# Weights of an input projection loaded and split in pairs of blocks, with two kinds of scratch tile in one ring of slots

## The chip, the cores and the metric

The kernel runs on one core of a Trainium2 chip. The metric is the device time of one launch in microseconds (us). Each engine of the core (PE for matmuls, ACT, DVE and POOL for everything elementwise, SP for issuing transfers) works through its own queue of instructions in order; they wait for one another by semaphores.

## What is computed

One layer of a streaming encoder on a sequence of 1024 tokens with 1024 channels, all in float32:

```
h   = RMSNorm(x) * (1 + scale(c)) + shift(c)
z   = h @ w_in          # 256 q latent, 128 kv latent, 32 rotary key, 3 x 512 for chunk attention
A   = latent attention, 8 heads: q and k, v expanded from the latents, rotary part, QK norm,
      softmax over all keys up to the query's chunk of 64
B   = chunk attention, 8 heads of 64: QK norm, relative position bias,
      softmax over the query's chunk and the 8 chunks before it
x1  = x + gate(c) * (concat(A, B) @ w_out)
out = x1 + gate2(c) * (silu(conv3(g)) * conv3(u)) @ w_down,   [g, u] = h2 @ w_up,  h2 = modulated RMSNorm(x1)
```

The channel sizes of the last line are 1024 to 2 x 2816 and 2816 to 1024. The change concerns only how `w_in` comes to be used.

## The kernel before, in words

Every float32 product is done as three matmuls: each operand is split into a rounded part (hi) and the rest (lo), and hi x hi, hi x lo and lo x hi are summed (`gemm3`, L146 to L152). A weight is thus loaded by SP, copied to its hi part by ACT (`hi_of`, L75), and its lo part is a subtraction on POOL (`lo_of`, L82).

The work has these stages, by time: the start to about 94 us (x is loaded and normed, scale and shift are computed, h is transposed, and the first q and k columns are projected); chunk attention to about 410 us, with the rest of the input projection between its tiles; latent attention to 684 us, first with the expansion of the latents and then with the first half of the output projection between its tiles; the second half of the output projection to 790; the MLP to the end.

The two attentions run over units (a head pair or a head, half of the queries) of four tiles of 128 queries. For each tile `scores` makes the scores (`sc` or `sm`, L658), ACT the exponentials (`Pc` or `Pm`, L683), POOL and DVE their two half-precision parts (`hlc` or `hlm`, L71 and L703), a DMA their transpose (`PTc` or `PTm`, L705); three tiles later `values` multiplies them with v (`pvc` or `pvm`, L716). Between these, `pace` draws steps from a list of generators, the fillers, in this order: v0, qk1, qk2, v1, qk3 (columns of chunk attention: `f_v`, `f_qk`), m (the latents: `f_m`), up0, up1 (`f_up`: expansion of the latents for four heads each) and oca (`f_oca`: the output projection's part of chunk attention). The program's text only says what is drawn when; a planner then orders every engine's queue at build time by its estimate of times, and also decides which slot of a pool a tile gets. A tile that gets a used slot makes its first writer wait for the last reader of the tile before.

`load_w` (L170 to L191) loads one such set of weights, in eight blocks of 128 channels. For 256 columns (`w_qk` as `wq_r`, `w_v` as `wv_r`) each block is one DMA of 128 KB (L184) into one of three raw slots of 128x256, one ACT copy (L75) and one POOL subtraction (L82) of 128x256. For the latents' 416 columns (`wm_r`) each block is a piece of 256 and one of 160 columns, each with its own DMA, copy and subtraction. Where v's norm is needed (`ssw`), ACT also squares each block (L187); the squares' sums go through `pow2_scale` (L337 to L352, PE's part `vsp` at L341) to the scale that v is multiplied with, and `vsp` stands ahead of the projection of v (`ipv`).

Two kinds of scratch tile matter. `rtile` (L134) gives a tile of 128x512 out of four slots named "R": `raw` in `qk_norm` (L363 to L375), `lat` in `f_m` (L472 to L503), `uqr` and `kraw` in `f_up` (L553 and L569), `cl` and `ch` in `f_oca`. `qtile` (L137) gives one of the same size out of two slots named "sq": the squares `sq`, `msq`, `usq` and the discarded squares `wv_j`, but also the raw weights of `f_up` (`wqr` L526, `wkr` L532) and of the output projection (`wor`, `load_wo`), and the results `co` of `f_oca` (L610) until they are stored.

Of the kernel before, what the change touches and what calls it, by code (L numbers as in the profile page):

```python
# [12 lines left out]
F32 = mybir.dt.float32  # L13
F32R = mybir.dt.float32r
# [3 lines left out]
AF = mybir.ActivationFunctionType  # L18
# [5 lines left out]
P = 128  # L24
# [3 lines left out]
ND = D // P  # L28
# [34 lines left out]
def layer_kernel(ctx, tc, I, out):  # L63
    nc = tc.nc
    pe, act, dve, pool, sp = nc.tensor, nc.scalar, nc.vector, nc.gpsimd, nc.sync

    def f32(ap):
        return ap.bitcast(F32)
# [4 lines left out]
    def hi_of(eng, o, i):  # L73
        if eng == "a":
            act.activation(o, i, AF.Copy)  # L75
        elif eng == "p":
            pool.tensor_scalar(o, i, 1.0, 0.0, op0=MUL, op1=ADD)
        else:
            dve.tensor_copy(o, i)

    def lo_of(eng, o, i, hi):
        (pool if eng == "p" else dve).tensor_tensor(o, i, f32(hi), op=SUB)  # L82
# [39 lines left out]
    hw = right.__enter__()  # L122
    att_pg = tc.tile_pool(name="apg", bufs=1, side="left")
    apg = att_pg.__enter__()
# [7 lines left out]
    st = startp.__enter__()  # L132

    def rtile(name, shape=(P, 512), dt=F32):  # L134
        return apg.tile(list(shape), dt, name=name, tag="R", bufs=4)

    def qtile(name):  # L137
        return apg.tile([P, 512], F32, name=name, tag="sq", bufs=2)

    def atile(name):  # L140
        return apg.tile([P, 256], F32, name=name, tag="A", bufs=3)
# [27 lines left out]

    def load_w(name, src, ncol, he="a", ssw=None):  # L170
        tiles = []
        for k in range(ND):
            if ncol <= 256:
                w = hw.tile([P, 2, 256], F32R, name=f"{name}s{k}", tag="ws", bufs=16)
                hi, lo = w[:, 0, :ncol], w[:, 1, :ncol]
            else:
                wh = hw.tile([P, 512], F32R, name=f"{name}h{k}", tag="ws", bufs=16)
                wl = hw.tile([P, 512], F32R, name=f"{name}l{k}", tag="ws", bufs=16)
                hi, lo = wh[:, :ncol], wl[:, :ncol]
            for c0 in range(0, ncol, 256):  # L180
                c = slice(c0, min(c0 + 256, ncol))
                raw = hw.tile([P, 256], F32, name=f"{name}r{k}_{c0}", tag="wr", bufs=3)
                rw = raw[:, :c.stop - c0]
                sp.dma_start(rw, src[:, k, c])  # L184
                if ssw is not None:
                    junk = qtile(f"{name}j{k}")
                    act.activation(junk[:, :c.stop - c0], rw, AF.Square, accum_out=ssw[:, k:k + 1])  # L187
                hi_of(he, hi[:, c], rw)
                lo_of("p", lo[:, c], rw, hi[:, c])
            tiles.append((hi, lo))  # L190
        return tiles  # L191


# [15 lines left out]
    for t in range(NT):  # L209
        xt = xs[t]  # L210
        junk = st.tile([P, D], mybir.dt.bfloat16, name=f"xj{t}", tag="hv", bufs=2)
# [20 lines left out]

    hT = {}
    wqk = load_w("wq0_", I["w_qk"][0], 256)
    qk0 = [ps.tile([P, 1024], F32, name=f"qk0_{i}", tag="S", bufs=2) for i in range(2)]
    for d in range(ND):
        if d + 1 < ND:
            load_ada(d + 1)
        w = wada[d]
# [15 lines left out]
        for t in range(NT):  # L255
            h, j = divmod(t, 4)
# [106 lines left out]
    def qk_norm(src_psum, nm, qn, j0):  # L363

        raw = rtile(f"raw{nm}")
        act.activation(raw[:], src_psum, AF.Copy)
        sq = qtile(f"sq{nm}")
        act.activation(sq[:], raw[:], AF.Square)
        ss = cst.tile([P, 8], F32, name=f"ss{nm}", tag="ss", bufs=4)
        r = cst.tile([P, 8], F32, name=f"r{nm}", tag="rr", bufs=4)  # L370
        dve.tensor_reduce(ss[:], sq[:].rearrange("p (a b) -> p a b", a=8), axis=AX.X, op=ADD)
        rsqrt_mean(r[:], ss[:], HD)
        pool.tensor_tensor(qn[:, j0:j0 + 2, :].rearrange("p t (a b) -> p (t a) b", a=4),
                           raw[:].rearrange("p (a b) -> p a b", a=8),
                           r[:].unsqueeze(2).to_broadcast([P, 8, HD]), op=MUL)  # L375
# [10 lines left out]
    def f_qk(p):  # L386
        w = load_w(f"wq{p}_", I["w_qk"][p], 256)
        for h in range(2):
            qns[p, h] = pgtile([P, 4, 256], F32, f"qn{p}_{h}")
        for t in range(0, NT, 2):  # L390
            pt = ps.tile([P, 512], F32, name=f"ipq{p}_{t}", tag="mm", bufs=2)
            yield from proj2(pt, t, w, 256)
            qk_norm(pt[:], f"{p}_{t}", qns[p, t // 4], t % 4)

    def f_v(pp):
        ssw = cst.tile([P, ND], F32, name=f"ssw{pp}")
        w = load_w(f"wv{pp}_", I["w_v"][pp], 256, ssw=ssw)
        vscale["c", pp] = pow2_scale(f"c{pp}", ssw[:], hb[:], ND, 2.0 * D)
        sc = vscale["c", pp][0]
        for t in range(0, NT, 2):  # L400
            h, j = divmod(t, 4)
            if j == 0:
                for i in range(2):
                    vts[2 * pp + i, h] = apg.tile([P, 4, 2, 2, 64], F16, name=f"v{2 * pp + i}_{h}", tag="v16", bufs=6)
            pt = ps.tile([P, 512], F32, name=f"ipv{pp}_{t}", tag="mm", bufs=2)
            yield from proj2(pt, t, w, 256)
            for i in range(2):
                vt = vts[2 * pp + i, h][:, j:j + 2]
                src = pt[:].rearrange("p (t q a b) -> p t q a b", t=2, q=2, a=2)[:, :, i]
                act.activation(vt[:, :, :, 0, :], src, AF.Copy, scale=sc)  # L410
                dve.scalar_tensor_tensor(vt[:, :, :, 1, :], src, sc, vt[:, :, :, 0, :], op0=MUL, op1=SUB)
# [105 lines left out]
    def f_up(gr):  # L517
# [24 lines left out]
        for t in range(NT):  # L542
            h, j = divmod(t, 4)
            sl = slice(j * P, (j + 1) * P)
            if t % 2 == 0:
# [4 lines left out]
            yield from gemm3_f(pt[:, :384], [(latT[k, h][:, 0, sl], latT[k, h][:, 1, sl], wq[k][:, 0, :384], wq[k][:, 1, :384])  # L550
                                for k in range(2)])
            raw = rtile(f"uqr{gr}_{t}")
            act.activation(raw[:, :384], pt[:, :384], AF.Copy)  # L553
            sq = qtile(f"usq{gr}_{t}")
# [261 lines left out]
    tiles = [(u, i) for u in units for i in range(4 * u.g, 4 * u.g + 4)]  # L816
    for n in range(len(tiles) + DEPTH):
        if n < len(tiles):
            u, i = tiles[n]
# [4 lines left out]
        if n >= DEPTH:  # L824
            u, i = tiles[n - DEPTH]
# [47 lines left out]
    for t in range(NT):  # L873
        lo = gb.tile([P, 4, P], F32R, name=f"ol{t}", tag="ol", bufs=3)
        hi = gb.tile([P, 4, P], F32R, name=f"oh{t}", tag="oh", bufs=3)
# [19 lines left out]
        if t % 4 == 3:  # L895
            h = t // 4
# [32 lines left out]
    def mt(tag, shape, name, dt=F32):  # L929
        return mp.tile(list(shape), dt, name=name, tag=tag, bufs=MB[tag])  # L930
# [21 lines left out]
    def split(src, nm):  # L952
        w = mt("ws", [P, 2, 512], nm, F32R)
        hi_of("a", w[:, 0], src)
        lo_of("p", w[:, 1], src, w[:, 0])
        return w
# [59 lines left out]
    for h in range(2):  # L1016
# [4 lines left out]
        for j in range(NF):  # L1021
            raw = mt("raw", [P, D], f"wd{h}_{j}")
            sp.dma_start(raw[:], I["w_down"][j * P:(j + 1) * P, :])
            dve.tensor_tensor(raw[:], raw[:], gmbc[:], op=MUL)  # L1024
            w = [split(raw[:, n * 512:(n + 1) * 512], f"wds{h}_{j}{n}") for n in range(2)]
# [11 lines left out]
        for t in range(4):  # L1037
            xt = mt("u", [P, D], f"xo{h}{t}")
            sp.dma_start(xt[:], x1_d[4 * h + t])
            for n in range(2):  # L1040
                c = slice(n * 512, (n + 1) * 512)
# [76 lines left out]
```

## Time and profile before

| | |
|---|---|
| runs | 1496.44, 1496.47, 1498.27 us; median 1496.47 |
| profiled execution | 1497.56 us, of which the span from first to last instruction is 1495.8 |
| mean granted clock of PE | 0.918 |
| busy in the span | PE 1283.1 us (86%), DVE 1037.7 (69%), POOL 841.8 (56%), ACT 617.5 (41%) |
| DMA | 185.94 MB, mean 124 GB/s |

"Busy" is the time in which an engine has an instruction in work. Matmuls are pipelined and their ends are modelled, so a PE that is busy all the time need not be at its peak; the granted clock, given as a share of full speed, tells whether it was held back. The timeline gives for each instruction its start, its duration, engine, line, operation and the tiles it writes and reads; in brackets stands how long the engine was idle before it and what released it. A window row gives the busy times of a stretch of the span.

### The profile page before, as it was taken

To read this page: it belongs to the slowest core of one execution; us is meant where nothing else is said; L and a number is where in the kernel's file an instruction comes from. 1 tells how busy PE (TensorE), PEld (TensorE's weight loads), DVE (VectorE), ACT (ScalarE), POOL (GpSimd) and SP (SyncE) were. 2 spreads that over 40 slices of the span, in tenths; PEclk is the share of its full clock that TensorE was granted. 3 is DMA by queue.
4 is the path that set the end of the run, shared out by engine and by line. 5 is a ranking of instruction groups with operands and counts; after the bars stand their busy time and mean duration, and the time that the engine had idled before them with its cause. 6 is when DMAs were issued, how large, how long until landed. Compare 5 with 4: busy or idle time off the path is not lost.

```text
span 1495.8 us, 20236 instructions
## 1 busy us (share of the span) xinstructions
PE 1283.1 (86%) x6836; PEld 1063.9 (71%) x6836; DVE 1037.7 (69%) x1710; ACT 617.5 (41%) x1190; POOL 841.8 (56%) x860
## 2 busy tenths in 40 slices
PE   3859989998968788876829769999999999999997
PEld 2759868976747666655617558888888887887885
DVE  6864786466768768863576658887787788556553
ACT  4454353343546545532444224444444443332331
POOL 4264453373799845443766146665565555665663
PEclk9979988998878899987958979999999999999999
DMA  7323656464512668778411242222222234446442
GB/s 275 134 70 73 135 121 143 116 134 102 124 49 53 145 144 167 163 156 287 149 74 57 71 143 82 85 85 85 85 85 84 77 129 169 148 148 234 154 141 99
DMA packets 217443, 185.94 MB, mean 124 GB/s; under 512 B 147958, under 2 KB 182906, under 8 KB 216316
## 3 DMA queue, kind: packets, MB, share of 16 engines
q1 hardware_dynamic: 217340, 184.66, 43.0%
q8 instruction: 54, 0.88, 0.2%
q14 instruction: 49, 0.40, 0.1%
HBM read 121.17 MB, written 28.84 MB: 100 GB/s over the span
## 4 chain that ended last, share of the span: by engine, by line
PE 48%; DMA 16%; DVE 13%; POOL 12%; issue 7%; ACT 2%; SPq 1%; DVEq 0%; POOLq 0%; ACTq 0%
PE p L964 7%; PE p L962 7%; PE p L963 7%; POOL wds L82 4%; DMA aw<-w_ada 4%; DMA PTm<-hlm 3%; PE sc L658 3%; PE dnp L1034 2%; PE dnp L1036 2%; PE dnp L1035 2%; DVE adacc L243 1%; DMA wu<-w_up 1%; PE ipv L150 1%; DVE aacc L430 1%; PE pvc L716 1%
## 5 line engine op out<-in xcount | busy, mean ns | idle before, releaser
L82 POOL TENSOR_TENSOR wds<-wd,wds 128x512 fp32r<-128x512 f32 x88 | 153.5, 1763 | 100.2 <-ACT wds L75 100.2
L1034 PE MATMUL dnp<-wds,g 128*128 128x512 f32 x308 | 119.9, 391 | 4.3 <-DVE xo L1042 2.4
L1024 DVE TENSOR_TENSOR wd<-wd,gmbc 128x1024 f32<-128x1024 f32 x44 | 69.4, 1578 | 77.7 <-DMA wd<-w_down 77.7
L1035 PE MATMUL dnp<-wds,g 128*128 128x512 f32 x308 | 119.7, 389 | 0.0
L1036 PE MATMUL dnp<-wds,g 128*128 128x512 f32 x308 | 118.5, 390 | 0.5 <-DVE g L82 0.5
L75 ACT ACTIVATE wds<-wd 128x512 fp32r<-128x512 f32 x88 | 54.6, 624 | 152.0 <-PE dnp L1036 149.6
L71 POOL TENSOR_SCALAR hlm<-Pm,rim 128x512 f16<-128x512 f32 (+4 forms) x88 | 61.7, 704 | 71.6 <-DMA PTm<-hlm 53.9
L703 DVE SCALAR_TENSOR_TENSOR hlm<-Pm,rim,hlm 128x512 f16<-128x512 f32 (+4 forms) x88 | 69.7, 795 | 31.7 <-POOL hlm L71 31.4
L71 POOL TENSOR_SCALAR hlc<-Pc,ric 128x640 f16<-128x640 f32 (+2 forms) x64 | 45.5, 713 | 77.9 <-DVE ric L686 38.7
L82 POOL TENSOR_TENSOR wc<-ws,wc 128x512 fp32r<-128x512 f32 x22 | 50.8, 2311 | 64.9 <-ACT wc L75 64.9
L82 POOL TENSOR_TENSOR wa<-wu,wa 128x512 fp32r<-128x512 f32 x22 | 35.9, 1633 | 91.1 <-ACT wa L75 91.1
L970 DVE SCALAR_TENSOR_TENSOR u<-c,pk,u 128x1023 f32<-128x1023 f32 x44 | 75.6, 1725 | 4.1 <-ACT u L969 4.1
L82 DVE TENSOR_TENSOR g<-gr,g 128x512 fp32r<-128x512 f32 x44 | 70.9, 1613 | 8.8 <-ACT g L75 8.8
L683 ACT ACTIVATE Pc<-sc,mc 128x640 f32<-128x640 f32 (+2 forms) x64 | 42.2, 659 | 83.6 <-DVE mc L673 66.9
L658 PE MATMUL sm<-mk,mq 96*128 96x512 f32 (+3 forms) x288 | 70.2, 378 | 7.0 <-ACT Pm L683 6.5
L716 PE MATMUL pvm<-PTm,vt 128*128 128x128 f16 x576 | 50.6, 242 | 29.4 <-DMA PTm<-hlm 25.3
L658 PE MATMUL sc<-k,q 64*128 64x512 f32 (+3 forms) x288 | 69.8, 370 | 5.6 <-ACT Pc L683 3.7
L430 DVE SCALAR_TENSOR_TENSOR aacc<-aw,cs,aacc 128x256 f32<-128x256 f32 x84 | 45.5, 541 | 41.8 <-DMA aw<-w_ada 41.2
L716 PEld LDWEIGHTS <-vt 128*128 128x128 f16 x576 | 41.2, 110 | 42.8 <-issue 40.0
L1034 PEld LDWEIGHTS dnp<-wds,g 128*128 128x128 f32 x308 | 57.8, 188 | 18.0 <-DVE xo L1042 3.3
L1036 PEld LDWEIGHTS dnp<-wds,g 128*128 128x128 f32 x308 | 57.8, 188 | 13.5 <-DVE g L82 1.4
L971 DVE SCALAR_TENSOR_TENSOR u<-c,pk,u 128x1022 f32<-128x1022 f32 x44 | 66.8, 1554 | 0.0
(352 smaller groups left out, 4350.8 us busy)
## 6 DMA issues: line engine op xcount, KB each, us to landing
wu<-w_up SPq DMA_DIRECT2D x44, 512.0 KB, 3.5
wd<-w_down SPq DMA_DIRECT2D x44, 512.0 KB, 3.5
aw<-w_ada SPq DMA_DIRECT2D x96, 128.0 KB, 2.3
g_d<-u SPq DMA_DIRECT2D x22, 512.0 KB, 2.6
gr<-g_d SPq DMA_DIRECT2D x44, 256.0 KB, 3.1
x<-x SPq DMA_DIRECT2D x16, 512.0 KB, 7.4
adaw<-w_ada_a SPq DMA_DIRECT2D x8, 1024.0 KB, 4.9
wq_r<-w_qk SPq DMA_DIRECT2D x32, 128.0 KB, 2.4
```

Of the source, the lines that this page charges most:

```text
L71: pool.tensor_scalar(o, i, s, 1.0, op0=MUL, op1=MUL)
L82: (pool if eng == "p" else dve).tensor_tensor(o, i, f32(hi), op=SUB)
L658: last = pe.matmul(s[:, c:c + w], qpg[rs_, a, q], kpgs[kh][rs_, b, ko:ko + w], start=(a == 0 and b == 0), stop=(a == 1))
L703: dve.scalar_tensor_tensor(hl[:, w:2 * w], pp, ri[:], hl[:, :w], op0=MUL, op1=SUB)
L716: last = pe.matmul(u.pv[:, c], u.vst(j), mov, start=(x == 0), stop=(x == len(todo) - 1))
L962: pe.matmul(pt, sh, pg[:, 0], start=(k == 0), stop=False)
L963: pe.matmul(pt, sh, pg[:, 1], start=False, stop=False)
L964: pe.matmul(pt, sl, pg[:, 0], start=False, stop=(k == 3))
L970: dve.scalar_tensor_tensor(u[:, 1:], c[:, :S - 1], pk[:, cv + 1:cv + 2], u[:, 1:], op0=MUL, op1=ADD)
L1034: pe.matmul(pts[t][n], sh, w[n][:, 0], start=(j == 0), stop=False)
L1035: pe.matmul(pts[t][n], sh, w[n][:, 1], start=False, stop=False)
L1036: pe.matmul(pts[t][n], sl, w[n][:, 0], start=False, stop=(j == NF - 1))
```

## The change

`load_w` treats two blocks of channels at a time when there are at most 256 columns, and one block of 416 columns whole otherwise. A raw tile is now 128x512 (two blocks of 256 columns side by side), with two slots in place of three of half the size. There is one DMA, one hi copy and one lo subtraction for a pair; the squares stay one for each block. The hi and the lo part are tiles of their own, of 128x512, in the same sixteen slots as before. The three raw slots of 1 KB in each partition become two of 2 KB. `rtile` and `qtile` now draw from one ring, "R", of five slots; before there were four and two. In the whole program ACT, POOL and SP have 32 instructions fewer each; PE and DVE have as many as before, in a new order in the stages up to the output projection.

```diff
     def rtile(name, shape=(P, 512), dt=F32):
-        return apg.tile(list(shape), dt, name=name, tag="R", bufs=4)
+        return apg.tile(list(shape), dt, name=name, tag="R", bufs=5)

     def qtile(name):
-        return apg.tile([P, 512], F32, name=name, tag="sq", bufs=2)
+        return apg.tile([P, 512], F32, name=name, tag="R", bufs=5)
...
     def load_w(name, src, ncol, he="a", ssw=None):
         tiles = []
-        for k in range(ND):
-            if ncol <= 256:
-                w = hw.tile([P, 2, 256], F32R, name=f"{name}s{k}", tag="ws", bufs=16)
-                hi, lo = w[:, 0, :ncol], w[:, 1, :ncol]
-            else:
-                wh = hw.tile([P, 512], F32R, name=f"{name}h{k}", tag="ws", bufs=16)
-                wl = hw.tile([P, 512], F32R, name=f"{name}l{k}", tag="ws", bufs=16)
-                hi, lo = wh[:, :ncol], wl[:, :ncol]
-            for c0 in range(0, ncol, 256):
-                c = slice(c0, min(c0 + 256, ncol))
-                raw = hw.tile([P, 256], F32, name=f"{name}r{k}_{c0}", tag="wr", bufs=3)
-                rw = raw[:, :c.stop - c0]
-                sp.dma_start(rw, src[:, k, c])
-                if ssw is not None:
-                    junk = qtile(f"{name}j{k}")
-                    act.activation(junk[:, :c.stop - c0], rw, AF.Square, accum_out=ssw[:, k:k + 1])
-                hi_of(he, hi[:, c], rw)
-                lo_of("p", lo[:, c], rw, hi[:, c])
-            tiles.append((hi, lo))
+        n = 2 if ncol <= 256 else 1
+        for k in range(0, ND, n):
+            raw = hw.tile([P, n, 512 // n], F32, name=f"{name}r{k}", tag="wr", bufs=2)[:, :, :ncol]
+            sp.dma_start(raw, src[:, k:k + n, :])
+            if ssw is not None:
+                for i in range(n):
+                    junk = qtile(f"{name}j{k + i}")
+                    act.activation(junk[:, :ncol], raw[:, i], AF.Square, accum_out=ssw[:, k + i:k + i + 1])
+            hi, lo = (hw.tile([P, n, 512 // n], F32R, name=f"{name}{x}{k}", tag="ws", bufs=16)[:, :, :ncol] for x in "hl")
+            hi_of(he, hi, raw)
+            lo_of("p", lo, raw, hi)
+            tiles += [(hi[:, i], lo[:, i]) for i in range(n)]
         return tiles
```

## The prediction

> **What bounds the kernel now.** I read the slices of the whole span first, then busy time by stage, then the timelines of the two stretches where PE stands still, then the waits by line. The slices show PE at 9 from slice 26 to the end but uneven before, and PEclk (the granted clock) in tenths:
>
> ```profile
> PE   3859989998968788876829769999999999999997
> POOL 4264453373799845443766146665565555665663
> PEclk9979988998878899987958979999999999999999
> ```
>
> The change touches nothing behind the output projection, so the last 706 us (790 to 1496, PE busy 666) stay as they are. What is left splits by the busy times of the stages (columns: PE busy and matmuls, weight loads, DVE, ACT, POOL, clock, DMA share, GB/s):
>
> ```profile
> 75.00:112.00 37.00, 21.30 (x132) 18.63 (x131) 24.32 (x81) 18.79 (x51) 23.22 (x29) 0.72 0.24 70
> 112.00:150.00 38.00, 38.00 (x308) 35.31 (x307) 17.68 (x51) 15.47 (x37) 15.72 (x22) 1.00 0.30 72
> 225.00:262.00 37.00, 36.66 (x249) 31.27 (x248) 24.50 (x89) 14.00 (x37) 13.41 (x19) 0.81 0.69 146
> ...
> 403.00:512.00 109.00, 81.35 (x438) 64.92 (x438) 84.09 (x215) 60.51 (x144) 103.24 (x191) 0.81 0.34 75
> 525.00:663.00 138.00, 115.37 (x792) 92.45 (x791) 104.11 (x258) 69.72 (x145) 62.66 (x73) 0.94 0.75 157
> ```
>
> While the input projection runs beside chunk attention, PE is full (38.00 of 38, 36.66 of 37) and POOL is at 36 to 41%. From 403 to 512, where the latents are expanded, POOL is the bound: 103.24 of 109. After that none is full, PE leads with 84%.
>
> **Work that goes, and why little of it counts.** Forty-eight blocks of w_qk and w_v become 24 pairs. A lo split of 128x256 on L82 takes 0.73 to 0.76 us, one of 128x512 1.27 to 1.28 (POOL's timeline): 2 x 0.745 - 1.28 = 0.21, times 24 = 5.0 us of POOL. The hi copies on L75 take 0.40 against 0.63: 0.17 x 24 = 4.1 us of ACT. w_m's pieces cost POOL 0.73 + 0.53; one of 416 columns, between the rows for 256 and 512, about 1.06: 0.2 x 8 = 1.6. SP issues 32 loads fewer, 0.33 to 0.5 us each, 11 to 16 us of its queue. All of it lies in stages that PE fills, so I count it at nothing; if PE were not the cover, the 6.6 us of POOL would be the most it could give. The same bytes move. 128 KB land in 2.3 to 2.6 us, 256 KB in 3.1 to 3.2, 512 KB in 3.5. What can count is who waits, at five places.
>
> **1. Start, 78 to 94.** PE stands 6.15, 4.86 and 3.58 us between its last qk matmul and the first v projection:
>
> ```profile
> 84.11 0.69 PE L618 MATMUL q_ps<-ident,qn 128*128 128x128 f32 x2 [6.15 <-POOL qn L373]
> 89.66 0.69 PE L618 MATMUL q_ps<-ident,qn 128*128 128x128 f32 x2 [4.86 <-POOL qn L373]
> 93.93 0.60 PE L341 MATMUL vspc<-vsc,ones 128*128 128x8 f32 x2 [3.58 <-DVE vsc L339]
> ```
>
> vspc needs the squares of all eight blocks of w_v. Five loads are issued only from 82.52 (8.18 us of SP), since three raw slots are held until the squares of the first blocks. Afterwards half the blocks are loaded ahead and two loads remain. Against it: the squares of qk_norm now take slots of the ring that its raw tiles hold (four raw tiles in five slots), so each waits for DVE's reduction; about 2 us later at the first free slot. Net -1.5 us; bounds -4 (the last square as soon as the normed qn, 89.66) and +2 (the slot waits alone).
>
> **2. v1's weights, 208 to 240.** This is the clearest stall:
>
> ```profile
> 215.31 2.29 PE L658 MATMUL sc<-k,q 64*128 64x128 f32 x6 [3.13 <-ACT Pc L683]
> ```
>
> ACT stood at 212.07 and 213.67 for wv_r with Pc queued behind; the load had been issued at 209.35, when the first square (208.31) freed its slot. The clock then stays at half:
>
> ```profile
> 200.00:208.00 8.00, 7.98 (x60) 6.53 (x60) 6.62 (x21) 3.78 (x9) 3.65 (x4) 1.00 0.51 122
> 208.00:216.00 8.00, 3.22 (x24) 2.45 (x24) 6.41 (x23) 5.74 (x21) 5.31 (x6) 0.74 0.63 140
> 216.00:224.00 8.00, 7.87 (x39) 6.31 (x39) 7.45 (x18) 4.35 (x12) 7.17 (x9) 0.50 0.61 128
> 224.00:232.00 8.00, 8.00 (x42) 6.82 (x42) 4.41 (x18) 1.83 (x5) 2.70 (x4) 0.50 0.80 158
> 232.00:240.00 8.00, 7.66 (x39) 6.62 (x36) 5.82 (x16) 5.35 (x13) 6.76 (x8) 0.55 0.72 167
> ```
>
> 39 to 42 matmuls in 8 us where there were 60. With pairs only two loads are late, the last lo split comes near 217.5 instead of 221.7, and in PE's new order vspc and the first 18 v matmuls stand ahead of the scores that wait. They fill part of the stall; the rest remains, since the first late load still waits for squares on ACT. I take -4 us (the 4.2 by which the splits are earlier). Bounds: 0, and -11: the 3.13 of idleness and the clock. From 216 to 240 there are 120 matmuls; at 60 per 8 us they take 16 us, not 24, so 8 us.
>
> Here the Trainium skill, TensorE: Matmul & The Clock Gate, Part 1, speaks against so large a gain: full rate is said to return after about 3.4 us of sustained work. By that rule removing the stall would save its 3.13 us and at most half of 3.4, no more than the forecast counts. The row disagrees: PE is marked busy 7.87 of 8 and the clock is 0.50 for two windows more. Such marks hold short waits, which may explain it; no row settles that.
>
> **3. The latents' expansion begins later, 386 to 405.** f_up(0)'s three weight loads take scratch slots. Before, they had the two slots of "sq", free at 386. Afterwards they are in the ring that lat_4 to lat_7 hold until their transposes. In SP's new order they come behind the transposes of the last chunk-attention tiles, and on PE the first qu stands behind PTc of the last tile, ahead of which it stood before.
>
> ```profile
> 390.87 1.00 POOL L82 TENSOR_TENSOR wq<-wqr,wq 128x384 fp32r<-128x384 f32 x1
> 392.63 1.64 POOL L82 TENSOR_TENSOR wq<-wqr,wq 128x384 fp32r<-128x384 f32 x1 [0.76 <-ACT wq L75]
> ...
> 398.42 1.54 POOL L82 TENSOR_TENSOR wk<-wkr,wk 128x512 fp32r<-128x512 f32 x1 [1.52 <-ACT wk L75]
> ```
>
> Now qu starts at 399.01 (PE's timeline) and POOL has hardly a gap from 402.3 on. lat_7 is normed at 389.4; its transposes end at 398.9. Loads that wait for them land 2.2 to 3.2 us later, and the hi and lo splits take about 2 us more: qu near 404.5, so +5.5 us. As the stage behind it is bound by POOL, this goes to the end of the stage; POOL's 5.8 us of gaps there (109 - 103.24) are the only cover. Bounds 0 and +8.
>
> **4. The ring in the POOL-bound stage.** Each tile takes three slots of five (uqr, usq, kraw) where it took two of four and one of two. From the timelines, uqr lives 8 to 20 us and kraw 5 to 18; four of them live at once for half of the stage, so ACT's copies already wait for POOL, which does not run dry. usq lives 1.1 to 2.9 us and fits into the fifth slot. +0.5, bounds 0 and +6 (POOL's 5.8 us of gaps there double).
>
> **5. oca and the tail, 500 to 684.** Its loads and its results share the ring too, so oca comes later in PE's order: some 24 oc matmuls move from about 650 into the tail, where the windows show PE idle behind DMA:
>
> ```profile
> 663.00:684.00 21.00, 7.48 (x60) 6.23 (x59) 6.46 (x8) 4.46 (x7) 8.03 (x9) 0.50 0.88 209
> ```
>
> At 0.39 each they free 24 x 0.25 = 6 us of PE's issue time ahead (they start 0.24 apart), in a stage that PE fills to 84%; in the tail they lie in gaps of 0.4 to 2.3 us. I take half, -3; bounds -6 and +3 (they wait on cl's 3.2 us landing, with pvm behind). The load of w_out goes the same way ahead of op0 (684.10, 4.74 idle behind ACT oh); 0, bounds -2 and +2.
>
> **Sum**: -1.5 - 4 + 5.5 + 0.5 - 3 + 0 = -2.5 us. The profiled execution took 1497.56 us (span 1495.8, 1.8 around it), 1.1 over the median of the runs, 1496.47: **1494.0**.
>
> **Rivals.**
> - The clock comes back (faster): place 2 gives its whole 11 and place 3 is half hidden by POOL's gaps (+2.5): -1.5 - 11 + 2.5 + 0.5 - 3 = -12.5, 1484. For: the half clock lasts 24 us behind one stall. Against: the first late load still waits for the squares.
> - The shared ring makes it slower: the ring orders weights, latents and squares one behind another at the latents' expansion. Place 3 costs 8, place 4 takes 4, place 5 gives nothing; places 1 and 2 give 3: +9, 1505.5. It decides as soon as wk's lo ends after about 404 (398.42 + 5.5), for then POOL starts the bound stage late with no gap left. For: the latents do hold the ring and POOL is 95% full. Against: uqr's copies wait for POOL already.
> - Nothing arrives (the change does not do what it says): the loads were hidden, delays and gains lie in gaps: 1496.5.
>
> **How the numbers follow.** A difference of 0.2% (3 us) is about what a measurement of this kernel can tell from none. Forecast 0.33 (own range 1489 to 1499), clock 0.22, ring 0.35, nothing 0.10. Faster than 1493.5: the clock's 0.22 and 0.16 of the forecast, together 0.38. Same: 0.16 of the forecast and 0.07 of nothing, 0.23. Slower: the ring's 0.35, 0.01 of the forecast and 0.03 of nothing, 0.39. The range that leaves 2 in 10 out reaches from 1482 (the clock's case with place 1 at its bound of -4) to 1510 (the ring's with place 4 at +6 and places 1 and 2 giving nothing: +14).
>
> **What would show it.** Place 1: vspc's start, near 92.4. Place 2: a shorter idle ahead of sc near 215 and the clock of 216 to 240. Place 3: wk's lo split, the first qu and POOL's last gap ahead of the bound stage. Place 4: POOL's busy share there, 95% now. Place 5: matmuls and clock in the last 21 us ahead of op. The forecast is wrong if another planner order creates a stall that none of these places has, above all a half clock of some 20 us as behind place 2.

## The result, and the profile after

| | before | changed |
|---|---|---|
| median | 1496.45 us | 1512.07 us (1508.94 to 1512.59) |
| ratio | | 1.0099, 95% interval 1.0077 to 1.0120 |
| profiled execution, span | 1497.56, 1495.8 | 1512.59, 1510.6 |

The change makes the kernel slower by 1%, some 15 us; the forecast was 1494.0 in a range of 1482 to 1510. Line numbers behind L184 are 7 lower in the changed kernel.

The slices of the changed kernel, to be held against those of before:

```profile
PE   3869989988767688785936849999999999999997
POOL 5254553463599933543866335566666654665663
PEclk9969989998787789996967969999999999999999
```

From slice 25 on PE is as full as before; what was lost was lost ahead of that. The start of the same events in both timelines tells where. In the names, `qu` is the first product of the latents' expansion, `pvm` the values of latent attention, `oc` the products of oca and `op` those of the output projection. Each difference counts from the start of the span, so it holds the ones ahead of it:

| event | before | changed | difference |
|---|---|---|---|
| scale of the first v (vsp, place 1) | 93.9 | 91.4 | -2.6 |
| scale of the second v (place 2) | 222.3 | 217.7 | -4.6 |
| last projection matmul of the second v | 272.4 | 267.3 | -5.1 |
| last scores of chunk attention | 394.1 | 393.2 | -0.9 |
| first qu (place 3) | 399.0 | 411.2 | +12.2 |
| 100th pvm (place 4) | 503.7 | 521.9 | +18.2 |
| first op (place 5) | 684.1 | 711.1 | +27.0 |
| 97th op | 718.0 | 735.0 | +17.0 |
| first matmul of the MLP | 786.7 | 803.6 | +16.9 |

**Places 1 and 2** together went as forecast: -5.5 us were counted, and -5.1 are there at the second v's last projection matmul, 2.5 of them from place 2. PE's gaps ahead of the first v are shorter (timeline of PE, changed kernel):

```profile
83.84 0.69 PE L611 MATMUL q_ps<-ident,qn 128*128 128x128 f32 x2 [4.47 <-POOL qn L366]
88.85 0.69 PE L611 MATMUL q_ps<-ident,qn 128*128 128x128 f32 x2 [4.32 <-POOL qn L366]
91.37 0.60 PE L334 MATMUL vspc<-vsc,ones 128*128 128x8 f32 x2 [1.84 <-DVE vsc L332]
```

The stall behind ACT's Pc is 1.34 us in place of 3.13, but a second one has come 14 us later:

```profile
214.18 2.29 PE L651 MATMUL sc<-k,q 64*128 64x128 f32 x6 [1.34 <-ACT Pc L676]
227.80 1.97 PE L651 MATMUL sc<-k,q 64*128 64x256 f32 x6 [3.33 <-ACT Pc L676]
```

The windows of this stretch (columns as in the prediction) show the clock back sooner than before, and then held back once more:

```profile
208.00:216.00 8.00, 5.14 (x20) 4.10 (x20) 7.13 (x20) 5.58 (x19) 5.76 (x6) 0.59 0.54 124
216.00:224.00 8.00, 8.00 (x52) 6.73 (x52) 6.30 (x16) 2.30 (x6) 6.50 (x7) 0.77 0.72 144
224.00:232.00 8.00, 4.67 (x34) 4.17 (x32) 6.66 (x25) 3.03 (x6) 4.20 (x4) 0.66 0.86 160
232.00:240.00 8.00, 8.00 (x62) 7.34 (x62) 5.31 (x15) 4.17 (x9) 3.73 (x4) 0.92 0.81 163
```

That is 168 matmuls in these 32 us where there were 144. Behind them most of the gain is lost again: in the stretch from 262 to 300 PE, 37.00 busy with 290 matmuls before, has 34.34 and 260, and at the last scores 0.9 us is left.

**Place 3.** The loads of f_up(0) are late as foreseen, and later. SP issues that of wk at 406.63 (391.89 before), as soon as it has issued the transpose of the last tile, and POOL's lo split of it, at 398.42 before, waits for it (SP's, then POOL's timeline of the changed kernel):

```profile
405.19 1.34 SPq L698 DMA_TRANSPOSE PTc<-hlc  x1
406.63 0.63 SPq L525 DMA_DIRECT2D wkr<-w_kvu  x1
```

```profile
410.88 1.28 POOL L82 TENSOR_TENSOR wk<-wkr,wk 128x512 fp32r<-128x512 f32 x1 [6.45 <-ACT wk L75]
```

PE has the last tiles of chunk attention ahead of the first qu now, and waits for their transposes. The last of them ends at 409.83; behind it comes vspm, which waits for a sum over wk's load, and then qu. So the tiles and the late load hold qu side by side, and the load less than 1 us longer:

```profile
404.69 1.22 PE L709 MATMUL pvc<-PTc,v 128*128 128x128 f16 x10 [2.90 <-DMA PTc<-hlc]
...
408.61 1.22 PE L709 MATMUL pvc<-PTc,v 128*128 128x128 f16 x10 [1.66 <-DMA PTc<-hlc]
410.74 0.58 PE L334 MATMUL vspm<-vsm,ones 128*128 128x1 f32 x2 [0.91 <-DVE vsm L332]
411.19 0.67 PE L150 MATMUL qu<-wq,latT 128*128 128x384 f32 x1
```

**Place 4.** The 109 us from where POOL is full:

```profile
415.00:524.00 109.00, 74.23 (x370) 58.53 (x369) 78.16 (x195) 57.33 (x138) 101.19 (x185) 0.79 0.25 55
```

POOL has 101.19 of 109 where it had 103.24, and PE 370 matmuls where it had 438.

**Place 5.** The waits by line between 500 and 712, PE alone, before and then changed (us in total, times, longest):

```profile
PE oc L150 <- ACT ch L75: 1.1, 2, 0.8
```

```profile
PE oc L150 <- ACT ch L75: 12.0, 9, 3.1
```

Each tile of oca is now loaded and split just ahead of its matmuls, and PE stands in front of them. At the end SP issues the transpose of the last tile right behind four loads of w_out of 256 KB each. PE has it 6.75 us after its issue, where the median of these transposes is 3.2, and stands meanwhile (SP's timeline, then PE's):

```profile
697.36 1.87 SPq L584 DMA_DIRECT2D wor<-w_out  x4
699.33 1.24 SPq L698 DMA_TRANSPOSE PTm<-hlm  x1
```

```profile
706.08 1.01 PE L709 MATMUL pvm<-PTm,vt 128*128 128x128 f16 x8 [6.51 <-DMA PTm<-hlm]
```

The output projection gives 10 us back: 144 matmuls in 34 us from its start, where there were 96. Its weights have all come by then, and PE has no stop in it, where before it stood 3.61 us for ACT oh and 2.02 for POOL ol:

```profile
684.00:718.00 34.00, 28.14 (x96) 21.49 (x97) 12.32 (x10) 8.14 (x15) 18.73 (x17) 0.81 0.79 281
```

```profile
711.00:745.00 34.00, 33.77 (x144) 27.30 (x145) 17.31 (x12) 8.34 (x15) 25.09 (x21) 0.95 0.82 293
```

### The profile page after: what moved, and what is told of

Its sections match the earlier page's. It is cut to its first block, busy times and chain, and to the rows that moved or that the text cites. A ratio compares the mean times of both kernels' runs of the same rounds, so it can differ in the third digit from the quotient of the medians.

```text
span 1510.6 us, 20082 instructions
## 1 busy us (share of the span) xinstructions
PE 1283.6 (85%) x6836; PEld 1065.9 (71%) x6836; DVE 1037.7 (69%) x1710; ACT 611.9 (41%) x1158; POOL 841.9 (56%) x828
## 4 chain that ended last, share of the span: by engine, by line
PE 29%; DVE 20%; DMA 19%; POOL 16%; issue 11%; ACT 3%; SPq 1%; DVEq 0%; POOLq 0%; ACTq 0%
DMA aw<-w_ada 5%; POOL wds L82 4%; DMA wu<-w_up 4%; DMA PTm<-hlm 3%; PE dnp L1027 2%; PE dnp L1029 2%; PE dnp L1028 2%; DVE wu L985 2%; DVE u L963 2%; PE sc L651 2%; DVE u L964 2%; PE p L957 2%; PE p L955 2%; PE p L956 2%; DVE adacc L236 2%
## 5 line engine op out<-in xcount | busy, mean ns | idle before, releaser
L82 POOL TENSOR_TENSOR wc<-ws,wc 128x512 fp32r<-128x512 f32 x22 | 55.9, 2542 | 83.4 <-ACT wc L75 83.4
L696 DVE SCALAR_TENSOR_TENSOR hlm<-Pm,rim,hlm 128x512 f16<-128x512 f32 (+4 forms) x88 | 65.4, 751 | 33.7 <-POOL hlm L71 33.2
L651 PE MATMUL sm<-mk,mq 96*128 96x512 f32 (+3 forms) x288 | 74.2, 390 | 11.5 <-ACT Pm L676 10.0
L709 PE MATMUL pvm<-PTm,vt 128*128 128x128 f16 x576 | 47.2, 233 | 32.8 <-DMA PTm<-hlm 32.6
L676 ACT ACTIVATE Pm<-sm,mm 128x128 f32<-128x128 f32 (+3 forms) x64 | 47.2, 738 | 52.5 <-DVE mm L670 25.3
```

What stands on the lines that cost most here:

```text
L651: last = pe.matmul(s[:, c:c + w], qpg[rs_, a, q], kpgs[kh][rs_, b, ko:ko + w], start=(a == 0 and b == 0), stop=(a == 1))
L676: act.activation(pr[:, :n], sv, AF.Exp, bias=m[:], scale=-1.0, accum_out=rsum[:, 0:1])
L696: dve.scalar_tensor_tensor(hl[:, w:2 * w], pp, ri[:], hl[:, :w], op0=MUL, op1=SUB)
L709: last = pe.matmul(u.pv[:, c], u.vst(j), mov, start=(x == 0), stop=(x == len(todo) - 1))
```

## The experiments

Each ratio is to the kernel before on the same chip, where its median was 1497.9 to 1500.6 us, and has its 95% interval behind it. Runs are best compared by these ratios. The starts of events come from one profiled execution of each kernel; executions of one kernel lie up to 16 us apart.

### Parts of the change, ordered by the planner

First theory: the ring makes the latents' expansion late, and oca with it. Rival: the pairs did it, through the order to which they led the planner.

**ring_only**: the ring of five in the kernel before.

```diff
-        return apg.tile(list(shape), dt, name=name, tag="R", bufs=4)
+        return apg.tile(list(shape), dt, name=name, tag="R", bufs=5)
...
-        return apg.tile([P, 512], F32, name=name, tag="sq", bufs=2)
+        return apg.tile([P, 512], F32, name=name, tag="R", bufs=5)
```

> The kernel before with one part of the change alone: rtile and qtile share one ring of five slots; load_w is as before. Theory (the ring makes the latents' expansion late, since f_up(0)'s raw weights wait for slots that latents hold): the first qu at 405 to 411 instead of 399.0, and 1504 to 1512 us in all. Rival (the pairs of blocks did it, by the order that they led the planner to): within 3 us of 1496.5, with qu at 398 to 401.

Measured 1518.82 us, ratio 1.0107 (1.0077 to 1.0137), first qu at 412.7. That is the theory's direction, and both lie just above its ranges.

**ring6_before**: the same with `bufs=6`.

> The kernel before with the ring shared, but six slots in it, as many as the two rings had together. If the lost slot is what costs: within 3 us of 1496.5. If the common order is what costs (a tile waits for whatever tile of the other kind had the slot): 1501 to 1510.

Measured 1527.64 us, ratio 1.0168 (1.0122 to 1.0214), more than either theory gave: more room does not make it faster. The qu is at 405.4, the first op at 718.8. So neither the lost slot nor the first qu alone explains the time.

**up_own**: the changed kernel, with two slots of their own for f_up's raw weights.

```diff
+    def gs(name):
+        return G["s"].tile([P, 512], F32, name=name, tag="Gs", bufs=2)
...
-            raw = qtile(f"wqr{gr}_{k}")
+            raw = gs(f"wqr{gr}_{k}")
...
-        raw = qtile(f"wkr{gr}")
+        raw = gs(f"wkr{gr}")
...
-        junk = qtile(f"wkj{gr}")
+        junk = gs(f"wkj{gr}")
```

> The changed kernel, with f_up's raw weights (and the discarded square of its k and v weights) in two slots of their own, in the room that the projection's weights have left by then; all other scratch in the ring of five. Theory of the late expansion: the first qu back at 398 to 403 (411.2 in the changed kernel), time down by 8 to 12 us, to 1500 to 1504. Rival (pairs, or the planner's new order around 265 to 360): 1509 to 1515, and qu no earlier than 407.

Measured 1521.20 us, ratio 1.0133 (1.0099 to 1.0167). The place went right and the time did not. The first qu is back, close behind wk (POOL's and PE's timelines):

```profile
400.33 1.26 POOL L82 TENSOR_TENSOR wk<-wkr,wk 128x512 fp32r<-128x512 f32 x1
```

```profile
401.61 0.67 PE L150 MATMUL qu<-wq,latT 128*128 128x384 f32 x1
```

but oca's last matmul comes at 708.0 (659.1 before), and the first op at 709.9. A gain of 10 us at 400 was given back later.

**both_own**: as up_own, and `load_wo`'s raw tile from `gs` too.

> The changed kernel, with f_up's and load_wo's raw weights in two slots of their own. Theory of the late expansion with oca's late weights as the second cost: 1493 to 1499, op starting at 685 to 695 instead of 711. If oca's weights cost nothing: as up_own within 3 us. Rival (pairs): 1509 to 1515.

Measured 1505.56 us, ratio 1.0038 (1.0014 to 1.0061): the fastest of all that the planner ordered, though its first qu is late again (405.2) and latent attention runs 19 us behind before; the output projection gains 10 of it. It lies between the ranges, and the first op, at 703.2, is later than the theory had it.

The times did not follow the places. So the second theory: it is the order of the queues that costs, and any edit of the pools gives the planner another one.

**late_own**: as both_own, and `usq` and `co` from `gs` too, so that from f_up on the slots are apart as they were before.

> The changed kernel, with all of qtile's tiles from f_up on (raw weights, usq, oca's results, w_out's raw weights) in two slots of their own, as before the change; the ring of five serves the rest and the stages ahead. Theory (the common ring costs twice, at the latents' expansion and where oca and w_out's loads queue for it): 1493 to 1500, qu at 398 to 403 and op at 682 to 692. Rival (the planner's order as such, any edit of the pools moves it by such amounts): 1505 to 1522.

Measured 1517.91 us, ratio 1.0113 (1.0095 to 1.0130), as the rival had it; the first qu is at 406.9 and the first op at 704.5.

**pairs_apart**: as late_own, with `rtile` on four slots of its own and `qtile` on one: pairs without any common ring.

```diff
-        return apg.tile(list(shape), dt, name=name, tag="R", bufs=5)
+        return apg.tile(list(shape), dt, name=name, tag="R", bufs=4)
...
-        return apg.tile([P, 512], F32, name=name, tag="R", bufs=5)
+        return apg.tile([P, 512], F32, name=name, tag="sq", bufs=1)
```

> Pairs of blocks without any shared ring: four slots for rtile and one for qtile up to f_up, then two for qtile as before the change. Theory (pairs alone gain at the start and at v1, the ring loses): 1489 to 1497. Rival (pairs or the planner's order lose): 1505 to 1520. If one slot for the squares chokes the start: vspc later than 95 and 1498 to 1504.

Measured 1524.77 us, ratio 1.0157 (1.0140 to 1.0174): the slots are apart and it is slower than with the ring.

**jit_before** and **jit_after**: a constant of the fillers' pace, in the kernel before and in the changed one.

```diff
-R_CA, R_MLA = 1.9, 0.5
+R_CA, R_MLA = 1.95, 0.5
```

> The kernel before with the filler's pace for chunk attention at 1.95 in place of 1.9, which changes no instruction, slot or transfer, only where the fillers are drawn and how the planner orders the queues. If an order as such moves the time little: within 4 us of before. Rival (any other order costs about as much as the change did): 8 to 20 us slower.

> The changed kernel with the same pace of 1.95. If the ring costs in every order: within 5 us of the changed kernel, 1507 to 1517. Rival (the changed kernel's order is an unlucky one): 1494 to 1503.

Measured 1514.27 us, ratio 1.0081 (1.0057 to 1.0105), and 1513.87, ratio 1.0084 (1.0058 to 1.0109). With slots, transfers and instructions as they were, the kernel before loses nearly what the change costs; the changed kernel loses nothing more. jit_after lies where the theory of the ring had it, but jit_before, without the ring, lies there too. All nine orders that the planner made after an edit, the changed kernel's among them, are 0.4 to 1.7% slower than the one of before.

### The order held

The next kernels hold the queues of all five engines to a given order by order-only edges between neighbours (no wait for an end). `ORDER` lists the instructions of an earlier kernel as they stood in its queues; those of `load_w` that have no counterpart find their own place.

```diff
+def pin(tc):
+    traced = {i.name: i for i in tc.nc.cur_bb.bb.instructions}
...
+                tc.add_manual_dep(traced[name], prev, mybir.DependencyInfo(
+                    mybir.DependencyClass.NoSync, mybir.DependencyReason.DATA), reason="pin")
...
         layer_kernel(ctx, tc, I, out)
+        pin(tc)
```

**pairs_held**: pairs_apart in the order of before.

> The pools and pairs of pairs_apart (no shared ring), with every queue held to the order of the kernel before; only the instructions of load_w find their own place. Theory (the planner's new order is what costs, the pairs themselves cost nothing or gain at the start and at v1): 1490 to 1499 where the same pools in the planner's own order took 1524.8. Rival (the pairs or the smaller slots cost in any order): 1508 or more.

Measured 1500.32 us, ratio 0.9998 (0.9982 to 1.0014), where the same pools took 1.0157 in the planner's own order. The order alone makes 1.6%, and the pairs with these pools neither cost nor gain as far as can be measured: vsp comes at 97.6 (one slot for four squares), and of those 4 us 1.7 are left at the first op, 685.8.

**late_own_held**: late_own in the order of before, but for the first norm of q and k.

> The pools of late_own (the ring of five up to f_up, two slots of qtile's own from there on, pairs), with every queue held to the order of the kernel before from the first norm of q and k on. Theory of the order: 1490 to 1499, where late_own took 1517.9 in the planner's order. Rival (the ring in the projection's stages costs by its waits): 1505 or more.

Measured 1503.80 us, ratio 1.0036 (1.0023 to 1.0049), where late_own took 1.0113; that lies between theory and rival. So a ring in the projection's stages costs a third of a per cent in that order: vsp is at 99.3.

**after_held**: the changed kernel, order of before where the ring allows it.

> The changed kernel, with the queues held to the order of the kernel before wherever the ring of five allows it: nearly all up to the first loads of f_up; there and through latent attention only some stretches, as the rest would lock up. If only the order costs: 1494 to 1500. If the ring costs where it forbids the order (f_up's loads, oca): 1501 to 1508, with qu at 402 or later. Rival (the ring's waits cost everywhere): 1510 or more.

Measured 1562.93 us, ratio 1.0426 (1.0405 to 1.0448). From the first qu (412.3) to the first op (747.8) it loses another 50 us. No theory had that. The order of before, in pieces, and the shared ring do not go together; how much of it is the ring's waits and how much the pieces' seams stays open. The order of before as a whole was not tried with the ring: by my reckoning the queues would lock up, which no run shows.

**late_new_order**: late_own in the order of the changed kernel.

> The pools of late_own, which have two slots of qtile's own from f_up on, with every queue held to the order of the changed kernel. If the order costs: 1508 to 1516, as the changed kernel. If what costs is waiting for slots of the ring while running: 1496 to 1503, as the slots are apart.

Measured 1524.48 us, ratio 1.0170 (1.0148 to 1.0193). With the slots apart from f_up on, the changed order still costs all of it and more. So it is not the waiting for the ring's slots in those stages that costs. Place 3 is late in it as well: wk's load, which is outside the ring here, is issued at 405.56 behind the same transpose, and the first qu comes at 410.1.

### Which stretch of the order

All with late_own's pools; the order of the changed kernel in one stretch, of before elsewhere. Ahead of the first v's scale all have the changed order.

**new_to_v0** is the base.

> The pools of late_own. Every queue in the order of the changed kernel up to the scale of the first v (vsp), and from there on in the order of the kernel before. This is the base for the three beside it. Theory (orders add up by stretches, and the start's gain of 2.6 us holds): 1493 to 1498. Rival (late_own's pools cost 4 us with any order of the start): 1500 to 1505.

Measured 1495.86 us, ratio 0.9990 (0.9974 to 1.0006).

**new_to_v1**: changed order to about 260 us.

> As new_to_v0, with the changed kernel's order up to the third quarter of the second v's projection (about 260 us). Theory (the gains that the prediction counted at the start and at v1's weights reach the end when nothing behind them is reordered): 1488 to 1494. Rival (what v1 gains is taken up behind it): within 3 us of new_to_v0.

Measured 1494.57 us, ratio 0.9982 (0.9968 to 0.9996). The interval ends just under 1: the gains at the start and at v1, 5.1 us where they arose in the changed kernel, are worth 2.7 us at the end, and this is the only kernel clear of the one of before on the faster side. With eighteen kernels compared, that one may be chance, and it is not told apart from new_to_v0.

**new_to_up**: changed order to the first qu.

> As new_to_v0, with the changed kernel's order up to the first qu, so over all of chunk attention and the input projection. If the loss arises in the order of latent attention alone: within 4 us of new_to_v1. If the last chunk-attention tiles ahead of f_up's first matmul are what costs (place 3 of the prediction): 8 to 12 us above new_to_v1.

Measured 1498.37 us, ratio 0.9994 (0.9977 to 1.0012). The changed order up to the latents' expansion costs nothing that can be measured. Place 3 is not in it, though: the last three tiles of chunk attention stand behind the first qu here (402.7), as they did before, so that half of its expectation is not tested by this kernel.

**new_in_mla**: changed order from the first qu to the first op.

> As new_to_v0, with the changed kernel's order again from the first qu to the output projection's first matmul. If the latents' expansion and latent attention hold the loss: 8 to 18 us above new_to_v0. If the loss is made ahead of f_up: within 4 us of new_to_v0.

Measured 1534.61 us, ratio 1.0243 (1.0216 to 1.0271), 2.5% above the base. The loss is here, and more than the changed kernel's own: from the first qu to the first op this kernel falls back by 27.1 us and late_new_order by 27.3, the changed kernel by 14.8. The changed order was made for the ring's slots, and with late_own's it costs more, so the sizes in this section are not those of the changed kernel.

**new_in_up** and **new_in_oca** share it out: from the first qu to the first oc, and from there to the first op.

> As new_to_v0, with the changed kernel's order from the first qu (the latents' expansion) to the first oc only; in the order of the kernel before again from the first oc on. If the expansion's order is the larger part (POOL, the bound there, stands between ropes behind f_up's and the ring's order): 15 us or more above new_to_v0. If oca's order is the larger part: 2 to 10 us.

> As new_to_v0, with the changed kernel's order from the first oc to the output projection only, where each oca tile is loaded and split just ahead of its matmuls. If that order (oc behind ACT ch and POOL cl, with scores and values queued behind oc) is the larger part: 15 us or more above new_to_v0. If the expansion is: 2 to 10 us. Additive stretches would give 38 together with new_in_up.

Measured 1524.81 us, ratio 1.0163 (1.0139 to 1.0188), and 1514.35, ratio 1.0104 (1.0066 to 1.0142). Against the base of 0.9990 that is 1.7% and 1.1%, 26 and 17 us, together 43 where new_in_mla had 38. So both count and add up nearly.

In new_in_up the weights are ready early: wk's lo split runs at 403.10, as POOL's timeline shows (lines are 8 to 11 higher in these kernels).

```profile
403.10 1.52 POOL L90 TENSOR_TENSOR wk<-wkr,wk 128x512 fp32r<-128x512 f32 x1 [2.25 <-ACT wk L83]
```

Yet the first qu comes at 417.14, since the changed order puts it behind the last three tiles of chunk attention, each of which waits for its transpose:

```profile
408.95 1.23 PE L720 MATMUL pvc<-PTc,v 128*128 128x128 f16 x10 [5.46 <-DMA PTc<-hlc]
412.05 1.23 PE L720 MATMUL pvc<-PTc,v 128*128 128x128 f16 x10 [1.87 <-DMA PTc<-hlc]
416.15 1.22 PE L720 MATMUL pvc<-PTc,v 128*128 128x128 f16 x10 [2.88 <-DMA PTc<-hlc]
417.14 0.67 PE L158 MATMUL qu<-wq,latT 128*128 128x384 f32 x1
```

In new_in_oca PE waits for oca's operands (waits by line, 500 to 715), which in the base takes 2.1 us:

```profile
PE oc L158 <- ACT ch L83: 10.3, 9, 2.7
```

```profile
PE oc L158 <- ACT ch L83: 2.1, 3, 1.1
```

How far the profiled executions are behind the one of before, in us:

| | first qu | 100th pvm | first op |
|---|---|---|---|
| changed | +12.2 | +18.2 | +27.0 |
| up_own | +2.6 | +9.9 | +25.8 |
| jit_before | +1.3 | +12.1 | +10.9 |
| pairs_apart | +5.2 | +13.9 | +18.4 |
| pairs_held | +4.1 | +4.8 | +1.7 |
| new_to_up | +3.7 | +3.6 | -0.3 |
| new_in_up | +18.1 | +33.5 | +31.5 |
| new_in_oca | +4.4 | +4.9 | +16.4 |

The queues left to the planner lose between the first qu and the 100th pvm, wherever the first qu stands: 5 to 17 us in all nine. Those with the order of before in that whole stretch lose less than 1.

## Why the prediction was wrong

The steps that failed are the prices of places 3 to 5, and the gains of places 1 and 2 taken to the end. The prices were read off rows in the order of before, while the change gives every queue a new order, in which the expansion and oca take longer. Forecast were -5.5 for places 1 and 2, +5.5 for place 3, +0.5 for place 4, -3 for place 5 and 0 for w_out. Measured were -0.9 as what is left of the first two, +13.1 up to the first qu, +6.0 up to the 100th pvm, +8.8 up to the first op and -10 in the output projection: +17.0, of which 14.8 are left in the span.

- **Work that goes, at nothing**: right. In the order of before, pairs are worth 0.9998 (0.9982 to 1.0014), which leaves little room for the 6.6 us of POOL.
- **Place 1** (-1.5): -2.6, inside its bounds. **Place 2** (-4): vsp is 4.6 earlier, but 2.6 of that came from place 1; the place itself gave 2.5 by the last matmul of v. That the sum of both came out at -5.1 is partly luck. A smaller stall was left, as foreseen; a second one, 3.33 us at 227.80, was not foreseen. The clock came back sooner, as the first rival had it, but without the 11 us. The estimate set against those 11 us, 3.13 and half of 3.4, comes to 4.8, a little above the 4 of the forecast and not below it.
- **The sum took these two to the end.** That step failed. Of 5.1 us at 267, 0.9 is left at 393. new_to_v1 puts their worth at the end at 2.7 us, and that only when the order behind them is the better one.
- **Place 3** (+5.5, at most 8): the positions were right, the price was not: from -0.9 at the last scores to +12.2. The step let the loads wait for the latents' transposes as they ended before, at 398.9, with qu starting when the weights are split. In the new order these transposes end at 406.9, between the last tiles; wk's load leaves SP at 406.63, behind the last tile's transpose; and the tiles themselves hold PE until 409.83. The prediction named both positions but gave them no price. late_new_order has the same delay with the load outside the ring, so it is the position and not the slot. What the tiles alone can cost, new_in_up shows: 12.5 us behind weights that are ready by 404.6.
- **Place 4** (+0.5, at most 6): +6.0, from first qu to 100th pvm, at its bound. The step asked whether slots would run out. late_new_order (12.4) and jit_before (10.7) lose more in this stretch with the slots apart: the order of the queues decides, and I had not compared that. Which part of the order it is, no run shows.
- **Place 5** (-3): wrong in sign. The oc matmuls did move into the tail, but with their loads and splits right ahead of them, so that PE waits 12.0 us for ch in place of 1.1; from the 100th pvm to the first op the loss is 8.8. I had named such waits as the upper bound, at +3. Of w_out (0, at most 2 either way) the wait for the last transpose behind four loads was real, 6.51 us, and the faster output projection gave 10 back, which the step had not counted.
- **The rivals.** The slower one named the ring, its place and 1505.5. Its direction was right and its reason half of it: up_own takes the weights out of the ring, mends place 3 and is no faster. What lacked was the rival that the experiments found, that the order of before is one which the planner did not find again after any of nine edits, worth 0.4 to 1.7%. The prediction had it only in its last sentence as a mishap, with no chance.

What stays open: why every other order of the planner is worse in the expansion. That qu stands behind the last tiles is one cause that the runs show; the loss between the first qu and the 100th pvm (10.7 us in jit_before, where qu is in time) is located in the order and not traced to an instruction. That the ring excludes the order of before is my reckoning, not shown by a run. Whether some order with the ring reaches the time of before is open as well: the pace was tried at one other value only.

## What to carry to other kernels

Where a planner orders the queues, a change of pools or loads changes the order of the whole program, and that can be worth more than all that the diff does: change an idle constant to learn how much an order as such is worth, then hold the order and measure the edit by itself. A gain in one stage counts only if the next bound stage starts earlier for it; here, of 5.1 us at 267, 0.9 was left at 393. And when a queue is reordered, price what the moved instruction now stands behind, as well as what it needs.

## What the runs showed of the chip

A pair of two 128 KB blocks lands later than one: in the DMA issues of the changed kernel

```profile
wq_r<-w_qk SPq DMA_DIRECT2D x16, 256.0 KB, 4.0
```

where 128 KB took 2.4. The pairs of w_v took 3.4 in place of 2.6. The forecast had taken 3.1 to 3.2 from other loads of 256 KB.

The clock around a stall differs between the two kernels. Before, finer windows show 1.00 from 211.0 to 211.9 and 0.50 from 212 to 239. So it had fallen by the time the stall of 3.13 us began, and it stayed down for 24 us behind it with PE marked busy 7.87 of 8 and 39 matmuls in a window. In the changed kernel it is 0.50 for the first 5.5 us behind the stall of 1.34 us, and full after that:

```profile
214.18:219.70 5.52, 5.52 (x25) 4.66 (x26) 5.30 (x10) 2.72 (x8) 5.27 (x5) 0.50 0.48 98
219.70:226.70 7.00, 4.77 (x38) 3.95 (x38) 5.34 (x20) 1.40 (x3) 3.73 (x4) 0.99 0.94 144
```

The Trainium skill, TensorE: Matmul & The Clock Gate, Part 1, states that about 3.4 us of sustained work bring full rate. The 5.5 us are somewhat longer than that, the 24 us far longer, and no run here tells what kept the clock down.
